# RG-LRU gate products of a hybrid decoder trunk: block-diagonal 128x128 weights replaced by 64x64 quadrants

## The chip, the core and the metric

The kernel runs on one NeuronCore of one Trainium2 chip. The metric is the device time of one execution in microseconds (us). Before the change the median of three runs was 1516.97 us (1516.93 to 1519.11). TensorE (PE in the rows; PEld its weight loads) multiplies into PSUM, VectorE (DVE) and ScalarE (ACT) work elementwise, SyncE (SP) issues transfers.

## The reference, cut to what matters

One step of a two-layer trunk, 1024 prompt positions and 8 decode tokens side by side (1032 columns), width 1024. Layer 0 holds an SSD mixer and a chunked gMLP, layer 1 a Conformer convolution module (C) and a Griffin RG-LRU (D). The change is in D, whose two gates are block-diagonal products with 16 heads of 64 channels:

```python
xc, buf_new = _causal_dwconv(xd, conv_buf, conv_w, conv_b)          # 4 taps
xb = xf.reshape(bsz, L, D_HEADS, D_BLOCK)                           # 16 heads of 64
r = sigmoid(einsum('blhi,hij->blhj', xb, wa).reshape(bsz, L, W) + ba)
i = sigmoid(einsum('blhi,hij->blhj', xb, wx).reshape(bsz, L, W) + bx)
log_a = -LRU_C * r * softplus(-lam)
a = exp(log_a);  bterm = sqrt(-expm1(2 * log_a)) * (i * xf)
h[t] = a[t] * h[t-1] + bterm[t]                                     # a scan over t
```

All arrays are fp32. C is a gated product, a causal convolution of 31 taps, a layer norm over the channels and SiLU; both branches are gated and go into one output projection.

## The kernel before, in words

Channels lie on the 128 partitions and the 1032 columns along the free axis, so each width of 1024 is eight blocks of 128 channels, and each block of D holds two heads. A large projection is a *unit* (line 120): 128 output channels in three column chunks of 344. `chunk` (line 107) writes one PSUM bank with 24 products: the fp32 operands are split into a high and a low part, and for each of eight contraction blocks lines 115 to 117 multiply high by high, high by low and low by high. The bank is then evacuated by ScalarE, or by VectorE for `ga` (line 827) and the output passes (line 732). `load_w` (line 93) brings a unit's weights, casts the high part on ScalarE (line 103) and subtracts on VectorE (line 104), at a raised priority of 700.

PSUM has eight banks of 512 fp32 columns: four under the tag "mm", which the chunks use, two under "sA" and two under "sB" for transposes, norms and gates (`bank`, line 59).

The program is written for a planner (the tile framework). It orders each engine's instructions by priority (program order, moved by `high_priority`) and by the times that its own timeline gives them, allots the slots of each tag, and places the semaphores. The engines then run these fixed orders, each waiting for what its next instruction needs.

Layer 1 runs as c, d, c, d and so on for eight blocks each (lines 903 to 905).

- `c_block(j)` (line 820): units `gb` and `ga`, the gated product `gl`, and `conv31` (line 841): 30 passes of VectorE over the block, one for each tap (line 859), 240 in all. They are put at priority -4000 and so fill what VectorE has left. `cacc` (line 865) sums the results over the blocks.
- `d_block(j)` (line 869): unit `xd` into `rwd`; `conv4` (line 291), one pass of ScalarE (line 294), three long passes of VectorE (line 297) and three of 8 columns for the decode tokens (line 300), into `xc`; unit `gd`; the gates; then the scan.

The gates before: two weight tiles `bd` (lines 809 to 818), each for four blocks, are zeroed by VectorE (line 812) and get their 64x64 diagonal blocks by 32 loads on SP's queue (line 817). Per block there are six products, two gates by three chunks, each 128x128 by 344 columns into the two "sA" banks, and a sigmoid behind each:

```python
for m, (t, bn) in enumerate(((rw, "lru_ba"), (gi, "lru_bx"))):          # L880
    for c in range(3):
        pg = bank("sA", f"gt{j}{m}{c}")                                  # L883
        T.matmul(pg[:, :CH], bd[:, m, j % 4, :], xc[:, cs], start=True, stop=True)
        S.activation(t[:, cs], pg[:, :CH], AF.Sigmoid, bias=pcol(bn, j)) # L885
```

In the trace a fp32 product is two instructions (passes), each with a weight load of its own.

After the eight blocks come eight units `gc`, meanwhile the results of D are reloaded (`mdl`) and split; then the output pass `od` over D (line 950) and `oc` over C (line 1013). While these run, the layer norm of C goes its way: the mean and the variance from `cacc` (lines 918 to 935), normalising and SiLU (lines 937 to 946), and the split into high and low operands, `hnh`/`hnl` for blocks 4 to 7 and `h_mc`/`l_mc` for blocks 0 to 3 (lines 949 and 953). `oc` multiplies blocks 4 to 7 first (k0=4). Its weights are `wh_oc`/`wl_oc`. After `oc` come the last norm and the outputs.

In layer 0 the SSD mixer has products of 64 output columns, `py` (lines 462 and 464): head h goes to PSUM partitions 0 to 63 or 64 to 127 by turns. `csT` (line 412) are products of 16 output columns, all on partitions 0 to 15. Both are fp32.

Of the kernel before, what the change touches and what calls it, by code (L numbers as in the profile page):

```python
# [10 lines left out]
AF = mybir.ActivationFunctionType  # L11
OP = mybir.AluOpType

P = 128
L = 1024
NS = 8
NT = L + NS
CH = NT // 3
NB = 8
# [4 lines left out]
RELU_ACT = 4  # L24
TPRI = 60
CPRI = 4000
ORDER = "cd" * 8

PROW = {}
# [15 lines left out]
def tile_trunk(ctx, tc, a, o):  # L45
    nc = tc.nc
    V, S, T, G, SY = nc.vector, nc.scalar, nc.tensor, nc.gpsimd, nc.sync
# [8 lines left out]
    def blk(tag, name, shape=None, dt=F32):  # L56
        return hp.tile(shape or [P, NT], dt, name=name, tag=tag, bufs=NTAG[tag])

    def bank(tag, name):
        return pp.tile([P, 512], F32, name=name, tag=tag, bufs=4 if tag == "mm" else 2)  # L60
# [59 lines left out]
    def unit(src, xs, name, evac, k0=0):  # L120
        w = load_w(src, name)
        for c in range(3):
            chunk(w, xs, c, name, evac, k0)
# [5 lines left out]
    def act_evac(dst, func, **kw):  # L129
        def f(ps, cs):  # L130
            S.activation(dst[:, cs], ps, func, **kw)  # L131
        return f

    def copy_evac(dst):
        def f(ps, cs):
            S.copy(dst[:, cs], ps)
        return f
# [43 lines left out]
    xts, ws = [], []  # L181
    for c in range(9):
# [7 lines left out]
        if c in (2, 3):  # L190
            col = XC + 1024 + (c - 2) * 256
# [46 lines left out]
    sc = cp.tile([P, NB, SR_BC], F32, name="sc")  # L238

    def pcol(name, j, k=0):  # L240
        return pc[:, j, PROW[name] + k:PROW[name] + k + 1]
# [38 lines left out]
    def tail_rows(t, lo, n, name, *outs):  # L280
        ps = bank("sA", "tl_" + name)
        T.transpose(ps[:n, :P], t[:, lo:lo + n], ident)
        rows = rowt("rows_" + name)
        S.copy(rows[:n], ps[:n, :P])
        i = 0
        for dst in outs:
            m = dst.shape[0]
            SY.dma_start(dst, rows[i:i + m])
            i += m

    def conv4(rw, dst, w, bcol, srow, j):
        pw, pb = PROW[w], PROW[bcol]
        col = lambda k: pc[:, j, pw + k:pw + k + 1]
        S.activation(dst, rw, AF.Identity, bias=pc[:, j, pb:pb + 1], scale=col(3))
        for k in range(3):
            d = 3 - k
            V.scalar_tensor_tensor(dst[:, d:L], rw[:, :L - d], col(k), dst[:, d:L], op0=OP.mult, op1=OP.add)
        st = sc[:, j, srow:srow + 24].rearrange("p (b k) -> p k b", k=3)
        for k in range(3):
            V.scalar_tensor_tensor(dst[:, L:], st[:, k, :], col(k), dst[:, L:], op0=OP.mult, op1=OP.add)  # L300

    def x_post(rw, col, j, bc, dst, name):
        conv4(rw, dst, "bc_w" if bc else "ssd_conv_w", "bc_b" if bc else "ssd_conv_b", S_BC if bc else S_SSD, j)
        S.activation(dst, dst, AF.Silu)
        tail_rows(rw, L - 3, 11, name, o["ssd_conv_prompt"][0, 0, :, col:col + P], o["ssd_conv_sample"][0, :, 2, col:col + P])
# [377 lines left out]
    def z_unit(j):  # L683
        t = blk("mt", f"sz{j}")
        unit(w_in_e[:, ZC + j * P:ZC + (j + 1) * P], hn, f"z{j}", act_evac(t, AF.Silu))
        V.tensor_mul(xy[j], xy[j], t)
        S.activation(t, xy[j], AF.Square)
        return t
# [13 lines left out]
    for g in range(2):  # L702
        acc = None
        for i in range(4):
            t = z_unit(g * 4 + i)
# [8 lines left out]
        for i in range(4):  # L714
            j = g * 4 + i
# [90 lines left out]
    V.tensor_scalar(cvec[:, :, 0], spl, -8.0, None, op0=OP.mult)  # L806
    V.tensor_scalar(cvec[:, :, 1], spl, 8.0, None, op0=OP.mult)

    bds = []
    for q, tag in enumerate(("S", "ws")):  # L810
        bd = blk(tag, f"bd{q}", [P, 2, 4, P])
        V.memset(bd, 0.0)
        for m, wn in enumerate(("lru_wa", "lru_wx")):
            for e in range(2):
                src = a[wn]
                for i in range(4):
                    SY.dma_start(bd[e * 64:(e + 1) * 64, m, i, e * 64:(e + 1) * 64], src[0, 2 * (q * 4 + i) + e])
        bds.append(bd)

    def c_block(j):  # L820
        sb = blk("xy", f"gl{j}")
        wb = load_w(w_in_o[:, GBC + j * P:GBC + (j + 1) * P], f"gb{j}")
        wa = load_w(w_in_o[:, GAC + j * P:GAC + (j + 1) * P], f"ga{j}")
        eb = act_evac(sb, AF.Sigmoid)

        def ea_(ps, cs):
            V.tensor_mul(sb[:, cs], ps, sb[:, cs])
        if j == 0:
            for c in range(3):
                chunk(wb, hn, c, f"gb{j}", eb)  # L830
                chunk(wa, hn, c, f"ga{j}", ea_)
        else:
            for c in range(3):
                chunk(wb, hn, c, f"gb{j}", eb)
            for c in range(3):
                chunk(wa, hn, c, f"ga{j}", ea_)
        js = slice(j * P, (j + 1) * P)
        tail_rows(sb, L - 30, 38, f"cc{j}", o["ccv_prompt"][0, 0, :, js], o["ccv_sample"][0, :, 29, js])
        conv31(j, sb)

    def conv31(j, gl):
# [13 lines left out]
        V.tensor_add(c[:, L:], c[:, L:], rd)  # L855
        with tc.high_priority(-CPRI):
            for k in range(29, -1, -1):
# [11 lines left out]
    def d_block(j):  # L869
        js = slice(j * P, (j + 1) * P)  # L870
        rw = blk("mt", f"rwd{j}")
        unit(w_in_o[:, XDC + j * P:XDC + (j + 1) * P], hn, f"xd{j}", copy_evac(rw))
        tail_rows(rw, L - 3, 11, f"lc{j}", o["lru_conv_prompt"][0, 0, :, js], o["lru_conv_sample"][0, :, 2, js])
        xc = blk("mt", f"xc{j}")
        conv4(rw, xc, "lru_conv_w", "lru_conv_b", S_LRUC, j)
        sgd = blk("ld", f"sgd{j}")
        unit(w_in_o[:, GDC + j * P:GDC + (j + 1) * P], hn, f"gd{j}", act_evac(sgd, AF.Silu))
        gi = blk("xx", f"gi{j}")
        bd = bds[j // 4]
        for m, (t, bn) in enumerate(((rw, "lru_ba"), (gi, "lru_bx"))):  # L880
            for c in range(3):
                cs = slice(c * CH, (c + 1) * CH)
                pg = bank("sA", f"gt{j}{m}{c}")  # L883
                T.matmul(pg[:, :CH], bd[:, m, j % 4, :], xc[:, cs], start=True, stop=True)
                S.activation(t[:, cs], pg[:, :CH], AF.Sigmoid, bias=pcol(bn, j))  # L885
        r = rw
        V.tensor_mul(gi, gi, xc)
        av = xc
        S.activation(av, r, AF.Exp, scale=cvec[:, j, 0:1])
        S.activation(r, r, AF.Tanh, scale=cvec[:, j, 1:2])  # L890
        hv = blk("mt", f"hv{j}")
        S.activation(hv, av, AF.Square)
        V.scalar_tensor_tensor(r, hv, 1.0, r, op0=OP.add, op1=OP.mult)
        S.activation(r, r, AF.Sqrt)
        V.tensor_mul(gi, gi, r)
        V.tensor_tensor_scan(hv[:, :L], av[:, :L], gi[:, :L], 0.0, op0=OP.mult, op1=OP.add)
        V.tensor_mul(hv[:, L:], av[:, L:], sc[:, j, S_LRU:S_LRU + NS])
        V.tensor_add(hv[:, L:], hv[:, L:], gi[:, L:])
        tail_rows(hv, L - 1, 9, f"lh{j}", o["lru_prompt"][0, :, js], o["lru_sample"][0, :, js])
        V.tensor_mul(hv, hv, sgd)  # L900
        SY.dma_start(mdd[j], hv)

    cj, dj = iter(range(NB)), iter(range(NB))
    for ch in ORDER:
        c_block(next(cj)) if ch == "c" else d_block(next(dj))
    sgc, md, mc = [], [None] * 8, [None] * 8
    for j in range(NB):
        t = blk("xy" if j < 7 else "S", f"sgc{j}")
        unit(w_in_o[:, GCC + j * P:GCC + (j + 1) * P], hn, f"gc{j}", act_evac(t, AF.Silu))
        sgc.append(t)  # L910
        if j >= 4:
            i = j - 4
# [9 lines left out]
    for i, j in enumerate((4, 5, 6, 7, 0, 1, 2, 3)):  # L922
        t = blk(("xy", "ce")[i % 2], f"cq{j}")
# [13 lines left out]
    for j in (4, 5, 6, 7, 0, 1, 2, 3):  # L937
        if j < 4:
            t = blk("bc", f"cr{j}")
            SY.dma_start(t, ccd[j])  # L940
            V.tensor_sub(t, t, mean)
        else:
            t = cs_t[j]
# [102 lines left out]
```

## Time and profile before

| | before |
|---|---|
| median of 3 runs | 1516.97 us (1516.93 to 1519.11) |
| profiled execution, first to last instruction | 1515.8 us (the profile shows nothing around it) |
| TensorE busy | 1497.5 us (99%), 9844 products |
| VectorE busy | 1058.3 us (70%) |
| ScalarE busy | 702.7 us (46%) |
| TensorE's granted clock, mean | 0.999 |

Busy time is the share of the span in which an engine ran an instruction. Products are pipelined: a record of TensorE is longer than the time to the next one's start, so what a product costs is read from starts, not from durations. In a timeline several equal instructions are merged (x4), with the start of the first and the time from there to the end of the last. "Idle before" says how long an engine waited and for whom. A line can be a helper's, so tiles are told by their names.

### The profile page before, as it was taken

The page shows a single profiled execution, that of the slowest core. Times are in us where ns is not written, and L with a number is a line of the kernel's source. Part 1 is how long each engine was busy: PE and PEld are TensorE (multiplying, and loading weights), DVE is VectorE, ACT ScalarE, POOL GpSimd, SP SyncE. Part 2 cuts the span into 40 slices and gives each one's busy share as a digit, 9 for nine tenths or more (in the row PEclk, how much of TensorE's full clock was granted, in tenths as well). Part 3 has the DMA queues.
Part 4 walks back from the last instruction along what each step waited for, and adds up shares of the span by engine and source line. Part 5 has one row for each costly group of instructions (what it writes and reads, how often), then busy time and mean ns, then how long its engine had stood idle before and what let it go on. Part 6 is the DMA issues. An engine that isn't in the chain of part 4 may idle for free.

```text
span 1515.8 us, 23657 instructions
## 1 busy us (share of the span) xinstructions
PE 1497.5 (99%) x9844; PEld 1464.1 (97%) x9844; DVE 1058.3 (70%) x1486; ACT 702.7 (46%) x1049; POOL 0.9 (0%) x7
## 2 busy tenths in 40 slices
PE   7999999999999999999999999999999999999998
PEld 6899999999999999999999999999999999999997
DVE  6535666568767862542437799999999999867524
ACT  6557666585654333420224445354445447334213
POOL 0000000000000000000000000000000000000000
PEclk9999999999999999999999999999999999999999
DMA  6225322233325661244432212221121221457402
GB/s 199 70 75 141 117 76 85 68 125 113 112 98 173 210 198 53 70 160 148 157 96 91 57 46 84 74 75 60 57 75 45 66 62 54 156 183 235 156 28 113
DMA packets 180193, 161.52 MB, mean 107 GB/s; under 512 B 11624, under 2 KB 159772, under 8 KB 180054
## 3 DMA queue, kind: packets, MB, share of 16 engines
q1 hardware_dynamic: 180086, 160.01, 33.5%
q8 instruction: 77, 1.26, 0.3%
q14 instruction: 30, 0.25, 0.1%
HBM read 118.91 MB, written 42.18 MB: 106 GB/s over the span
## 4 chain that ended last, share of the span: by engine, by line
PE 97%; ACT 1%; DVE 1%; DMA 0%; issue 0%; SPq 0%; DVEq 0%
PE mm_x L115 2%; PE mm_xd L115 2%; PE mm_x L117 2%; PE mm_xd L117 2%; PE mm_ob L116 2%; PE mm_od L115 2%; PE mm_z L115 2%; PE mm_oa L115 2%; PE mm_z L117 2%; PE mm_x L116 2%; PE mm_od L116 2%; PE mm_gd L115 2%; PE mm_u L115 2%; PE mm_ob L115 2%; PE mm_g L115 2%; PE mm_oc L115 2%
## 5 line engine op out<-in xcount | busy, mean ns | idle before, releaser
L859 DVE SCALAR_TENSOR_TENSOR c<-gl,pc,c 128x1017 f32<-128x1017 f32 (+25 forms) x240 | 294.7, 1262 | 0.9
L116 PE MATMUL mm_gb<-hnl,wh_gb 128*128 128x344 f32 x192 | 63.5, 331 | 0.3 <-DVE hnl L127 0.3
L115 PE MATMUL mm_gb<-hnh,wh_gb 128*128 128x344 f32 x192 | 63.1, 329 | 0.3 <-ACT gl L131 0.3
L115 PE MATMUL mm_xd<-hnh,wh_xd 128*128 128x344 f32 x192 | 62.6, 326 | 0.7 <-ACT wh_xd L103 0.7
L115 PE MATMUL mm_ga<-hnh,wh_ga 128*128 128x344 f32 x192 | 63.3, 329 | 0.0
L115 PE MATMUL mm_u<-hnh,wh_u 128*128 128x344 f32 x192 | 62.6, 326 | 0.0
L117 PE MATMUL mm_gb<-hnh,wl_gb 128*128 128x344 f32 x192 | 62.4, 325 | 0.0
L115 PE MATMUL mm_v<-hnh,wh_v 128*128 128x344 f32 x192 | 62.4, 325 | 0.0
L117 PE MATMUL mm_ga<-hnh,wl_ga 128*128 128x344 f32 x192 | 62.4, 325 | 0.0
L117 PE MATMUL mm_v<-hnh,wl_v 128*128 128x344 f32 x192 | 62.2, 324 | 0.0
L116 PE MATMUL mm_v<-hnl,wh_v 128*128 128x344 f32 x192 | 62.1, 324 | 0.0
L116 PE MATMUL mm_ga<-hnl,wh_ga 128*128 128x344 f32 x192 | 62.1, 324 | 0.0
L116 PE MATMUL mm_gc<-hnl,wh_gc 128*128 128x344 f32 x192 | 62.0, 323 | 0.0
L117 PE MATMUL mm_x<-hnh,wl_x 128*128 128x344 f32 x192 | 62.0, 323 | 0.0
L115 PE MATMUL mm_gc<-hnh,wh_gc 128*128 128x344 f32 x192 | 61.9, 323 | 0.0
L117 PE MATMUL mm_xd<-hnh,wl_xd 128*128 128x344 f32 x192 | 61.9, 324 | 0.0
L115 PE MATMUL mm_x<-hnh,wh_x 128*128 128x344 f32 x192 | 61.9, 322 | 0.0
L117 PE MATMUL mm_gd<-hnh,wl_gd 128*128 128x344 f32 x192 | 61.8, 322 | 0.0
L116 PE MATMUL mm_x<-hnl,wh_x 128*128 128x344 f32 x192 | 61.8, 322 | 0.0
L116 PE MATMUL mm_u<-hnl,wh_u 128*128 128x344 f32 x192 | 61.7, 321 | 0.0
L115 PE MATMUL mm_g<-hnh,wh_g 128*128 128x344 f32 x192 | 61.7, 321 | 0.0
L116 PE MATMUL mm_g<-hnl,wh_g 128*128 128x344 f32 x192 | 61.7, 321 | 0.0
(476 smaller groups left out, 4932.5 us busy)
## 6 DMA issues: line engine op xcount, KB each, us to landing
x<-res SPq DMA_DIRECT2D x16, 516.0 KB
csb<-csd SPq DMA_DIRECT2D x16, 512.0 KB
mbd<-u SPq DMA_DIRECT2D x8, 516.0 KB
mbl<-mbd SPq DMA_DIRECT2D x8, 516.0 KB
rb<-res SPq DMA_DIRECT2D x8, 516.0 KB
res<-rb SPq DMA_DIRECT2D x8, 516.0 KB
res<-x SPq DMA_DIRECT2D x8, 516.0 KB
mdd<-hv SPq DMA_DIRECT2D x8, 516.0 KB
```

The lines of the kernel that those rows point to most:

```text
L115: T.matmul(out, wh[:, k, :], xh[:, cs], start=i == 0, stop=False)
L116: T.matmul(out, wh[:, k, :], xl[:, cs], start=False, stop=False)
L117: T.matmul(out, wl[:, k, :], xh[:, cs], start=False, stop=i == NB - 1)
L859: V.scalar_tensor_tensor(c[:, d:L], gl[:, :L - d], w(k), c[:, d:L], op0=OP.mult, op1=OP.add)
```

## The change

Each gate product of 128x128 with two zero blocks becomes two products of 64x64, one for each head. The tile `gwt` holds the blocks without zeros and is filled by four loads. A block's twelve products stand one after another at a priority raised by 200 and write six banks: two of "mm", two of "sB", two of "sA". Row half e of the operands writes the bank e of its chunk; gate a goes to the same half of the output partitions, gate x to the other one. Twelve sigmoids of 64 partitions read them, those of gate a first. In `conv4` the three short passes go ahead of the three long ones.

```diff
+GPRI = 200
@@ conv4
+        st = sc[:, j, srow:srow + 24].rearrange("p (b k) -> p k b", k=3)
+        for k in range(3):
+            V.scalar_tensor_tensor(dst[:, L:], st[:, k, :], col(k), dst[:, L:], op0=OP.mult, op1=OP.add)
         for k in range(3):
             d = 3 - k
             V.scalar_tensor_tensor(dst[:, d:L], rw[:, :L - d], col(k), dst[:, d:L], op0=OP.mult, op1=OP.add)
-        st = sc[:, j, srow:srow + 24].rearrange("p (b k) -> p k b", k=3)
-        for k in range(3):
-            V.scalar_tensor_tensor(dst[:, L:], st[:, k, :], col(k), dst[:, L:], op0=OP.mult, op1=OP.add)
@@ weights of the gates
-    bds = []
-    for q, tag in enumerate(("S", "ws")):
-        bd = blk(tag, f"bd{q}", [P, 2, 4, P])
-        V.memset(bd, 0.0)
-        for m, wn in enumerate(("lru_wa", "lru_wx")):
-            for e in range(2):
-                src = a[wn]
-                for i in range(4):
-                    SY.dma_start(bd[e * 64:(e + 1) * 64, m, i, e * 64:(e + 1) * 64], src[0, 2 * (q * 4 + i) + e])
-        bds.append(bd)
+    gwt = blk("S", "gwt", [P, 2, NB, 64])
+    for m, wn in enumerate(("lru_wa", "lru_wx")):
+        src = a[wn][0].rearrange("(j e) i o -> e i j o", e=2)
+        for e in range(2):
+            SY.dma_start(gwt[e * 64:(e + 1) * 64, m], src[e])
+
+    def gates(j, xc, r, gi):
+        rows = [slice(e * 64, (e + 1) * 64) for e in range(2)]
+        pgs = [[bank(tag, f"gt{j}{c}{e}") for e in range(2)] for c, tag in enumerate(("mm", "sB", "sA"))]
+        with tc.high_priority(GPRI):
+            for c in range(3):
+                cs = slice(c * CH, (c + 1) * CH)
+                for m in range(2):
+                    for e in range(2):
+                        T.matmul(pgs[c][e][rows[e ^ m], :CH], gwt[rows[e], m, j, :], xc[rows[e], cs], start=True, stop=True)
+        for m, (t, bn) in enumerate(((r, "lru_ba"), (gi, "lru_bx"))):
+            for c in range(3):
+                cs = slice(c * CH, (c + 1) * CH)
+                for e in range(2):
+                    S.activation(t[rows[e], cs], pgs[c][e][rows[e ^ m], :CH], AF.Sigmoid, bias=pcol(bn, j)[rows[e]])
@@ d_block
-        bd = bds[j // 4]
-        for m, (t, bn) in enumerate(((rw, "lru_ba"), (gi, "lru_bx"))):
-            for c in range(3):
-                cs = slice(c * CH, (c + 1) * CH)
-                pg = bank("sA", f"gt{j}{m}{c}")
-                T.matmul(pg[:, :CH], bd[:, m, j % 4, :], xc[:, cs], start=True, stop=True)
-                S.activation(t[:, cs], pg[:, :CH], AF.Sigmoid, bias=pcol(bn, j))
+        gates(j, xc, rw, gi)
```

## Rows read from the trace of the kernel before

**Rows 1.** The page: busy time (share of the span) by engine; the chain by engine.

```profile
PE 1497.5 (99%) x9844; PEld 1464.1 (97%) x9844; DVE 1058.3 (70%) x1486; ACT 702.7 (46%) x1049; POOL 0.9 (0%) x7
...
PE 97%; ACT 1%; DVE 1%; DMA 0%; issue 0%; SPq 0%; DVEq 0%
```

**Rows 2.** Tile `gt`: duration in ns min/median/max, first and last start in us, forms.

```profile
L884 PE MATMUL gt<-xc,bd x96: 450/452/459, 876.1 to 1256.7; 128*128 128x344 f32 x96
L885 ACT ACTIVATE rwd<-gt,pc x24: 541/548/552, 876.8 to 1252.7; 128x344 f32<-128x344 f32 x24
```

**Rows 3.** Timeline of TensorE at the first gate products: start, us, instruction.

```profile
876.07 1.32 PE L884 MATMUL gt<-xc,bd 128*128 128x344 f32 x4
876.97 0.58 PE L117 MATMUL mm_gb<-hnh,wl_gb 128*128 128x344 f32 x1
877.38 0.32 PE L115 MATMUL mm_gb<-hnh,wh_gb 128*128 128x344 f32 x1
```

**Rows 4.** Timelines of TensorE at `py` and `csT`; last, `py`'s weight loads by tile.

```profile
157.59 0.32 PE L115 MATMUL mm_C<-hnh,wh_C 128*128 128x344 f32 x1
157.84 1.09 PE L462 MATMUL py<-csb,x 128*64 128x128 f32 x16
158.86 0.50 PE L470 MATMUL pn<-x,bth 128*128 128x512 f32 x1
...
75.52 1.05 PE L412 MATMUL csT<-tri,dA 128*16 128x128 f32 x8
...
L462 PEld LDWEIGHTS py<-csb,x x256: 132/137/137, 157.8 to 450.3; 128*64 128x64 f32 x128
```

**Rows 5.** Timeline of ScalarE around the first block's sigmoids.

```profile
873.90 1.05 ACT L103 CAST wh_ga<-wr_ga 128x1024 fp32r<-128x1024 f32 x1 [3.17 <-PE mm_gd L116]
875.33 1.28 ACT L885 ACT_TABLE_LOAD   x1
878.99 0.46 ACT L131 ACTIVATE gl<-mm_gb 128x344 f32<-128x344 f32 x1 [1.02 <-PE mm_gb L117]
```

**Rows 6.** Busy time in stretches of 50 us, then PEclk, DMA share, GB/s.

```profile
870.00:920.00 50.00, 50.00 (x311) 48.61 (x310) 47.83 (x48) 25.48 (x34) 0.00 (x0) 1.00 0.25 78
1120.00:1170.00 50.00, 50.00 (x311) 48.59 (x311) 48.34 (x50) 23.55 (x33) 0.00 (x0) 1.00 0.22 67
1270.00:1320.00 50.00, 50.00 (x320) 49.93 (x319) 47.40 (x43) 21.36 (x30) 0.00 (x0) 1.00 0.40 125
```

**Rows 7.** The page's convolution group; timelines of VectorE and TensorE at block 5's gates.

```profile
L859 DVE SCALAR_TENSOR_TENSOR c<-gl,pc,c 128x1017 f32<-128x1017 f32 (+25 forms) x240 | 294.7, 1262 | 0.9
...
1130.71 0.22 DVE L300 SCALAR_TENSOR_TENSOR xc<-sc,pc,xc 128x8 f32<-128x8 f32 x1
...
1136.52 1.03 PE L884 MATMUL gt<-xc,bd 128*128 128x344 f32 x3
```

**Rows 8.** Timelines of VectorE, TensorE and ScalarE from `cacc` to the start of `oc`.

```profile
1323.22 1.23 DVE L865 TENSOR_TENSOR cacc<-cacc,c 128x1032 f32<-128x1032 f32 x1
...
1374.38 1.23 DVE L104 TENSOR_TENSOR wl_od<-wr_od,wh_od 128x1024 fp32r<-128x1024 f32 x1 [0.41 <-ACT wh_od L103]
...
1383.47 0.51 DVE L732 TENSOR_TENSOR rd<-mm_od,rd 128x344 f32<-128x344 f32 x1
...
1396.60 1.22 DVE L127 TENSOR_TENSOR hnl<-sgc,hnh 128x1032 fp32r<-128x1032 f32 x1
...
1413.56 4.66 DVE L127 TENSOR_TENSOR l_mc<-sgc,h_mc 128x1032 fp32r<-128x1032 f32 x4
...
1409.35 0.32 PE L115 MATMUL mm_oc<-hnh,wh_oc 128*128 128x344 f32 x1
...
1415.00 0.64 PE L115 MATMUL mm_oc<-h_mc,wh_oc 128*128 128x344 f32 x3
...
1417.52 0.32 PE L116 MATMUL mm_oc<-l_mc,wh_oc 128*128 128x344 f32 x1
...
1409.43 1.05 ACT L103 CAST wh_oc<-wr_oc 128x1024 fp32r<-128x1024 f32 x1 [1.42 <-PE mm_od L116]
1410.39 3.91 ACT L126 CAST h_mc<-sgc 128x1032 fp32r<-128x1032 f32 x4
```

**Rows 9.** Tile `bd`: loads on SP's queue and the memsets, as in rows 2.

```profile
L817 SPq DMA_DIRECT2D bd<-in_lru_wa_dram x16: 475/594/728, 827.1 to 842.4; - x16
L812 DVE MEMSET bd<- x2: 912/912/912, 826.2 to 827.3; 128x1024 f32 x2
```

## The prediction

> **What bounds the kernel now.** I read the busy shares first, then the chain that ended last, then the gate products by their tile and in the order of time, then the other engines around them. TensorE is busy for 1497.5 of 1515.8 us and 97% of the chain is TensorE [rows 1]: a TensorE instruction taken away shortens the run, unless something else has been hiding just behind it. The gate products are 96 instructions (48 products, two passes each) [rows 2]. Four of them start at 876.07; the next projection product but one starts at 877.38, and a projection product takes 0.157 (36 of them lie between 1409.35 and 1415.00 [rows 8]), so four passes hold TensorE for 1.31 - 0.157 = 1.15 us, 0.289 us each [rows 3]. That is two cycles a column for 344 columns at the granted full clock. In all 96 x 0.289 = 27.7 us, all on the path: 3.47 us in each of the eight blocks.
>
> The second thing to see is VectorE: busy 47.8, 48.3 and 47.4 of 50 us in stretches from 870 to 1320 us [rows 6], because the 240 convolution passes of line 859 [rows 7], 30 to a block and put last in priority, fill every gap. It is nearly a second bound.
>
> **The change part by part.**
>
> *Products.* A block's 6 products (12 passes) become 12 quadrant products (24 passes), each with the same 344 columns, so 0.289 us each. What a block costs depends on how many run at once. No row shows 64-row operands. The nearest rows are those of `py`: 64 output columns, alternately in the lower and the upper column half. Sixteen passes of 128 columns span 1.09 us; less the 0.27 of the last record, that is 15 steps of 0.055. Eight `csT` passes, all in one column half, have steps of (1.05 - 0.27) / 7 = 0.111 for the same 128 columns [rows 4]. So two column halves do run beside each other. The ends for a block: one at a time 24 x 0.289 = 6.94; two at a time 3.47; four at a time 1.73. I take four: the row halves read different partitions, and the change gives each row half a PSUM bank of its own.
>
> Changing between whole-array and divided products costs something: `py` starts 0.25 after the product before it instead of 0.157, and the product after its last pass (157.84 + 1.09 - 0.27 = 158.66) starts 0.20 later instead of 0.11 [rows 4], together 0.19 per block if the twelve stay together. New cost 1.73 + 0.19 = 1.92, saved 3.47 - 1.92 = 1.55 per block, **12.4 us** in all on TensorE.
>
> The Trainium skill (TensorE: Matmul & The Clock Gate, "What overlaps and what doesn't") says that a weight load overlaps running matmuls only where its row group differs. By that rule loads within a row half would stand between the passes. The `py` passes share all rows, and a pair's 0.11 has no room for a load recorded at 0.137 [rows 4], so this trace does not bear the rule out.
>
> *Sigmoids.* Six of 0.548 us on 128 partitions [rows 2] become twelve on 64. No row has the narrow form; between half (0.27) and the whole I take the whole, since a row of the same length streams as many columns. That adds 6 x 0.55 = 3.3 us of ScalarE per block, where it is busy about 24 of 50 us [rows 6]. Hidden beside the projections; what it delays is the release of the banks (a rival below) and `gi`, which nothing soon needs.
>
> *Banks.* Two of the four "mm" banks, both "sB" and both "sA" are held per block. A projection chunk is 24 x 0.157 = 3.8 us and uses one mm bank. The first two banks are free after the eighth sigmoid: about 0.6 + 1.28 (table load [rows 5]) + 8 x 0.55 = 6.3 us. The other two mm banks take 7.6 us of products. I cost this at nothing; the cover is thin.
>
> *Weights.* 32 loads of about 0.59 us on SP's queue and two memsets of 0.91 us on VectorE go; four loads come [rows 9]. The loads are between 4 x 0.48 = 2 and the old 19 us. Either way they land well ahead of 876, with the weight loads queued behind them on SP earlier, not later. Zero: the projections hide it. The "ws" slot set free has no waiting user; zero, and the memsets' 1.8 us are spent before the convolution backlog exists.
>
> *conv4 order.* The three small passes (0.22 us) go ahead of the three long ones. Same instructions; `xc` may be ready up to 0.7 us sooner or later per block, against a lead of 5.6 (below). Zero.
>
> *What is late next.* The convolution passes end with `cacc` at 1323.22. From there a chain of layer norm work leads to the operands of pass `oc`: `hnl` 1397.8, `h_mc` from 1411.4 to 1414.3, `l_mc` up to 1418.2 [rows 8]. TensorE reaches `oc` at 1409.35 and needs `l_mc` at 1417.52, where it had first done other chunks' products on `hn`: this is met with little to spare. VectorE's work before `cacc` does not shrink, so the chain stays where it is while TensorE comes 12.4 us sooner, at 1397.0. Then four open banks give 4 x 12 x 0.157 = 7.5 us of `hn` products, to 1404.5, and TensorE waits for `h_mc`. With the chain unmoved the four chunks' remaining 48 products end shortly after 1418.2, at about 1418.2 + 4 x 0.157 = 1418.8. Now they end at 1409.35 + 96 x 0.157 = 1424.4. So the gain left is **5.6 us**; 6.8 are given back.
>
> Bounds of the chain's shift: 2.8 later (TensorE ahead pulls one more unit's VectorE work, 1.23 + 3 x 0.51 [rows 8], in front of `cacc`), or up to 6.8 sooner if VectorE's waits go. Some of these are waits for TensorE, as the 1.42 us of ScalarE before `wh_oc` at 1409.43 [rows 8]. I take no shift.
>
> *Sum.* The profiled span of 1515.8 lies 1.2 below the median of the runs, 1516.97; I carry the 1.2. 1516.97 - 12.4 + 6.8 = **1511.4**, this case's own range 1504.6 to 1514.2.
>
> **The rivals.**
>
> *The order no longer fits (same to slower).* The planner writes VectorE's queue by its own costs. Should it count the 24 passes one after another, it sees 6.9 us where it now sees 3.5, and puts three more convolution passes (3 x 1.17 us) per block ahead of that block's `xc`. In block 5 `xc` is ready at 1130.9 and used at 1136.5, a lead of 5.6 [rows 7]; it is gone after two blocks, and TensorE then waits for `xc`. A block is 12 x 3.77 + 3.47 = 48.7 us on TensorE; VectorE's 47.8 per 50 is 46.6 in it, plus 3.5 = 50.1, so 8 x 1.4 - 5.6 = about +5 us: 1522, between 1517 and 1525. The later passes then have less to wait for, so no loss at `oc`. For it: VectorE's share. Against: it needs a wrong cost that no row shows. 0.20.
>
> *Banks (slower).* At a block's twelve, if ScalarE puts all twelve sigmoids, the table load and two casts of 1.05 [rows 5] ahead of the next chunk's evacuation (0.46), the bank returns after 6.6 + 1.3 + 2.1 + 0.5 = 10.5 us against 7.6 of cover: 2.9 us idle a block, 23 in all, 1516.97 - 12.4 + 23 = 1527.6. It turns slower where the loss passes 1.55 us a block. For it: two banks fewer. Against: ScalarE is half idle, and the needed banks come back at the eighth sigmoid. 0.12.
>
> *Only two at a time.* 3.47 + 0.19 per block: +1.5, 1518.5. `py` shows no more than two. 0.08.
>
> *One after another* (the change does not do what it says): 6.94 + 0.19 - 3.47 = 3.66 per block, 1546. `py` speaks against. 0.05.
>
> *Weight loads exposed within a row half.* 12 loads of 0.137 per row half, the halves side by side, add 1.6 per block: 3.6 against 3.47, 1518. This is what the skill's rule on row groups would do. 0.03.
>
> **How the numbers follow.** The forecast has 0.52. About 0.2% (3 us) is what a measurement here can tell from no change: faster is below 1513.9, slower above 1520. Faster: 0.50 (the forecast, without its upper end). Same: 0.02 + 0.08 (the order, where it costs little) + 0.08 + 0.03 = 0.21. Slower: 0.12 (the order otherwise) + 0.12 + 0.05 = 0.29. The range from 1504 to 1526 takes in the forecast's bounds, the order and most of the banks' case; it leaves out 0.05 for one after another and some 0.08 more.
>
> **What would show it.** Gate passes in groups of 24 that take about 1.9 us (four at a time), 3.5 (two) or 6.9 (one); blocks some 1.5 us shorter on TensorE; VectorE still about 95% busy and `cacc` still near 1323; TensorE waiting on `h_mc` or `l_mc` for some 5 to 7 us at the start of `oc`. Waits of gate passes on `xc` would speak for the order; waits of `mm_gb` or `mm_ga` on a sigmoid or an evacuation, for the banks. I am wrong if TensorE's path shrinks by 12 us with no wait at `oc` (about 1505), or if the twelve do not overlap at all.

## The result and the profile after

The changed kernel takes 1576.5 us (1575.6 to 1577.1) against 1516.97: ratio 1.039, 95% interval 1.038 to 1.040. It is slower, and above the predicted range. The profiled execution spans 1574.7 us, 58.9 more than before. The line numbers have moved by up to some 15.

The page after the change: busy time by engine, the chain by engine, and one of the costliest groups (busy us, mean ns).

```profile
PE 1504.5 (96%) x9940; PEld 1469.2 (93%) x9940; DVE 1061.7 (67%) x1484; ACT 737.9 (47%) x1103; POOL 0.9 (0%) x7
...
PE 80%; ACT 9%; DVE 8%; issue 2%; DMA 0%; SPq 0%; DVEq 0%; ACTq 0%
...
L117 PE MATMUL mm_ga<-hnl,wh_ga 128*128 128x344 f32 x192 | 67.6, 352 | 0.0
```

TensorE now sits idle for 1574.7 - 1504.5 = 70.2 us, where it was 18.3 [rows 1]: 51.9 more. The other 7.0 are busy time, although the gates became cheaper, and a projection product has a mean of 352 ns in `mm_ga` where `mm_u` shows 321 to 326 on the same page. Both come from the same waits, as the rows below show. TensorE's waits after the change (what it waited for: us in total, times, longest):

```profile
PE tl_lh L283 <- DVE hv L907: 41.1, 8, 6.8
PE gt L828 <- DVE xc L301: 9.9, 6, 3.2
```

Neither wait was there before. The first is of a product that the change doesn't touch: `tl_lh`, the transpose of the last rows of the scan's result `hv`. Block 3 on TensorE (start, us, instruction, idle before it and releaser):

```profile
1038.47 0.32 PE L118 MATMUL mm_gd<-hnh,wl_gd 128*128 128x344 f32 x1
1040.64 1.97 PE L828 MATMUL gt<-xc,gwt 64*64 64x344 f32 x24 [1.84 <-DVE xc L301]
1042.53 0.43 PE L116 MATMUL mm_gb<-hnh,wh_gb 128*128 128x344 f32 x1
...
1057.27 0.32 PE L116 MATMUL mm_ga<-hnh,wh_ga 128*128 128x344 f32 x1
1063.12 0.37 PE L283 MATMUL tl_lh<-ident,hv 128*9 128x128 f32 x1 [5.54 <-DVE hv L907]
...
1063.59 0.49 PE L118 MATMUL mm_ga<-hnh,wl_ga 128*128 128x344 f32 x1
1063.87 0.49 PE L116 MATMUL mm_ga<-hnh,wh_ga 128*128 128x344 f32 x1
```

All 24 passes stand together and take 1.97, so four run at once, as predicted. But the gates now come straight behind the last product of `gd`, with no projection between, in all eight blocks; before, 14 to 173 projections stood there. They wait for `xc`; then 94 products and 15 us later TensorE stands still for `hv`, with 50 ready products of `ga` behind the transpose in its queue. VectorE and ScalarE in the same stretch:

```profile
1039.21 1.27 DVE L301 SCALAR_TENSOR_TENSOR xc<-rwd,pc,xc 128x1023 f32<-128x1023 f32 x1
...
1041.54 7.82 DVE L874 SCALAR_TENSOR_TENSOR c<-gl,pc,c 128x1016 f32<-128x1016 f32 x6
...
1060.64 2.28 DVE L905 TENSOR_TENSOR_SCAN hv<-xc,gi 128x1024 f32<-128x1024 f32 x1
1062.84 0.14 DVE L907 TENSOR_TENSOR hv<-hv,gi 128x8 f32<-128x8 f32 x1
```

```profile
1041.52 1.28 ACT L833 ACT_TABLE_LOAD   x1 [1.45 <-PE gt L828]
1042.81 0.54 ACT L833 ACTIVATE rwd<-gt,pc 64x344 f32<-64x344 f32 x1
...
1049.52 1.28 ACT L898 ACT_TABLE_LOAD   x1
```

From the gates to `hv` it is 1062.98 - 1040.64 = 22.3 us: twelve sigmoids up to 1049.5, four passes of ScalarE with table loads between them, and VectorE's part of the chain, with eleven convolution passes put among it. Before, `hv` came later still, 26 to 36 us behind the first gate product, but 117 to 191 products stood between the last gate product and the transposes, so that TensorE never waited there.

What a stall does to the clock stands in the busy time by stretch (from:to, length, busy of PE, PEld, DVE, ACT, POOL, then the granted clock, DMA share, GB/s):

```profile
1043.00:1057.00 14.00, 14.00 (x91) 14.00 (x90) 13.57 (x12) 13.73 (x19) 0.00 (x0) 1.00 0.12 36
1060.00:1063.00 3.00, 0.00 (x0) 0.00 (x0) 3.00 (x4) 1.34 (x3) 0.00 (x0) 0.59 0.00 0
1063.00:1066.00 3.00, 2.88 (x11) 2.91 (x12) 3.00 (x3) 0.26 (x1) 0.00 (x0) 0.50 0.00 0
1069.00:1072.00 3.00, 3.00 (x21) 3.00 (x20) 2.96 (x4) 0.00 (x0) 0.00 (x0) 1.00 0.28 109
```

During the 5.5 us in which TensorE did nothing the granted clock fell to 0.50, the level of 1.2 GHz, and stayed there behind the stall: products start 0.28 to 0.29 apart (1063.59, 1063.87 and on) instead of 0.157. So a stall is paid for twice.

VectorE over the whole stage shows what gave way:

```profile
1020.00:1070.00 50.00, 42.62 (x270) 41.08 (x269) 48.19 (x46) 27.03 (x38) 0.00 (x0) 0.93 0.22 67
1320.00:1370.00 50.00, 50.00 (x320) 50.00 (x319) 6.14 (x5) 11.56 (x20) 0.00 (x0) 1.00 0.18 53
```

It is as full as before [rows 6], but with other work. Convolution passes started before the gates of blocks 0 to 7 (counted in the trace): 12, 39, 65, 90, 118, 144, 173, 202 before; 12, 38, 67, 97, 127, 157, 187, 217 after. From block 2 on that is 30 a block: every block's whole convolution is done inside one round of the loop, no backlog is left for the time behind the last gates, where VectorE is now free (6.14 of 50 us), and a round takes 54 to 59 us instead of 49 to 56.

### The profile page after: what moved, and what is told of

The parts are those of the page before. It is cut to its first block, busy times and chain, and to the rows that moved or that the text cites. A ratio compares the mean times of both kernels' runs of the same rounds, so it can differ in the third digit from the quotient of the medians.

```text
span 1574.7 us, 23857 instructions
## 1 busy us (share of the span) xinstructions
PE 1504.5 (96%) x9940; PEld 1469.2 (93%) x9940; DVE 1061.7 (67%) x1484; ACT 737.9 (47%) x1103; POOL 0.9 (0%) x7
## 4 chain that ended last, share of the span: by engine, by line
PE 80%; ACT 9%; DVE 8%; issue 2%; DMA 0%; SPq 0%; DVEq 0%; ACTq 0%
DVE c L874 4%; PE mm_x L116 2%; PE mm_x L118 2%; PE mm_ob L117 2%; PE mm_od L118 2%; PE mm_z L116 2%; PE mm_od L116 2%; PE mm_oa L116 2%; PE mm_z L118 2%; PE mm_x L117 2%; PE mm_oc L116 2%; PE mm_ob L116 2%; PE mm_u L116 2%; PE mm_g L116 2%; PE mm_oa L118 2%; PE mm_oa L117 2%
## 5 line engine op out<-in xcount | busy, mean ns | idle before, releaser
L874 DVE SCALAR_TENSOR_TENSOR c<-gl,pc,c 128x1015 f32<-128x1015 f32 (+20 forms) x240 | 299.4, 1265 | 2.7
L117 PE MATMUL mm_ga<-hnl,wh_ga 128*128 128x344 f32 x192 | 67.6, 352 | 0.0
L118 PE MATMUL mm_ga<-hnh,wl_ga 128*128 128x344 f32 x192 | 67.5, 352 | 0.0
L116 PE MATMUL mm_ga<-hnh,wh_ga 128*128 128x344 f32 x192 | 66.6, 347 | 0.0
L118 PE MATMUL mm_gc<-hnh,wl_gc 128*128 128x344 f32 x192 | 62.6, 326 | 0.0
L118 PE MATMUL mm_u<-hnh,wl_u 128*128 128x344 f32 x192 | 61.6, 321 | 0.0
L116 PE MATMUL mm_z<-hnh,wh_z 128*128 128x344 f32 x192 | 61.6, 321 | 0.0
```

The costliest lines, as they stand in the source:

```text
L116: T.matmul(out, wh[:, k, :], xh[:, cs], start=i == 0, stop=False)
L117: T.matmul(out, wh[:, k, :], xl[:, cs], start=False, stop=False)
L118: T.matmul(out, wl[:, k, :], xh[:, cs], start=False, stop=i == NB - 1)
L874: V.scalar_tensor_tensor(c[:, d:L], gl[:, :L - d], w(k), c[:, d:L], op0=OP.mult, op1=OP.add)
```

## The experiments

The theory: the two banks taken from "mm" are what costs. Slots of a tag are allotted in program order. With two of the gates' banks between the chunks of `gd` and of `gb`, no chunk of `gb` comes ahead of a block's gates, and TensorE is tied to `xc` in each block. The counts in the traces bear this out: no projection stands between `gd` and the gates, in any block, in the changed kernel and the four others below that have the gates' banks at this place, and 14 to 194 in those whose gates take none from "mm". Before, the gates slid back behind up to 173 projections, and VectorE lived on that lead. Rivals: the raised priority, the quadrants with their twelve sigmoids, the order in `conv4`, the length of the chain to `hv`.

**The priority.**

```diff
-GPRI = 200
+GPRI = 0
```

> The changed kernel with the products' raised priority set to 0, all else kept. Theory (the two banks taken from the projections' tag tie the projections to the gates of their block; the priority has no part in it): within 3 us of the changed kernel's 1576.5, TensorE waiting some 41 us in all for hv and some 10 us for xc as in the changed kernel. Rival (the raised priority pulls the gates forward onto xc): the waits for xc and for hv fall below 10 us together, and the time goes to 1505 to 1520.

Measured: 1576.7 us, the waits the same.

```profile
PE tl_lh L283 <- DVE hv L907: 42.5, 8, 6.8
PE gt L828 <- DVE xc L301: 9.8, 5, 2.6
```

The raised priority has no part in it.

**Quadrants without "mm".**

```diff
-enumerate(("mm", "sB", "sA"))
+enumerate(("sA", "sB", "sA"))
```

> The changed kernel with its first pair of banks taken from sA instead of the projections' tag mm (so sA, sB, sA), the raised priority kept. Theory (the mm banks are the cause): projection chunks stand between gd and the gates again, TensorE's waits for xc and hv fall from 51 us to under 10, the granted clock returns to about 0.99 or more, and the time is 1505 to 1522: 1517 less the 12 to 13 us of gate time, plus up to 5 for passes that no longer stay together and up to 7 given back at oc. Rival (the quadrants or the twelve narrow sigmoids are the cause, whatever bank they use): the waits for hv stay above 25 us and the time above 1550.

Measured: 1516.7 us, ratio 0.9995 (0.9985 to 1.0004). Of TensorE's two waits one is left:

```profile
PE tl_lh L283 <- DVE hv L907: 1.0, 1, 1.0
```

The banks are the cause: the same quadrants and sigmoids on other banks, 15 to 112 projections between `gd` and the gates again, and 60 us are gone. That it is the place of the banks and not their number, the later runs show. Nothing was won over the kernel before, though. Four banks hold only eight of the twelve products, so the passes come in groups of 16, 4 and 4. TensorE at block 1's gates:

```profile
926.95 0.32 PE L117 MATMUL mm_gb<-hnl,wh_gb 128*128 128x344 f32 x1
927.20 1.39 PE L828 MATMUL gt<-xc,gwt 64*64 64x344 f32 x16
928.52 0.42 PE L118 MATMUL mm_gb<-hnh,wl_gb 128*128 128x344 f32 x1
928.78 0.32 PE L116 MATMUL mm_gb<-hnh,wh_gb 128*128 128x344 f32 x1
```

The first group takes 928.78 - 926.95 - 2 x 0.157 = 1.52 us: four steps of 0.289 and 0.36 for the two changes between whole and divided products. The groups of four passes (both products on one row half, so two at a time) take 0.92 each by the same reckoning. 1.52 + 2 x 0.92 = 3.36 against 3.47 before: the switching eats the gain.

**The transposes later.** In the changed kernel:

```diff
-        tail_rows(hv, L - 1, 9, f"lh{j}", ...)
+        with tc.high_priority(-150):
+            tail_rows(hv, L - 1, 9, f"lh{j}", ...)
```

> The changed kernel with one edit: the transposes of the last rows of hv are put 150 lower in priority, so that some 143 projection products instead of 95 stand between the gates and them. Theory (TensorE stands in order behind these transposes until hv is ready, 41 us in all, and the clock lost after it costs some 20 more): 48 more products at 0.157 are 7.5 us of cover against waits of at most 6.8, so the waits for hv vanish, the waits for xc stay at 10 us or grow somewhat, and the time is 1512 to 1535. Rival (the wait for hv only shows a lag of VectorE, which will be met elsewhere): as much idle time turns up in waits for xc or for banks, and the time stays within 15 us of 1576.

Measured: 1567.9 us, the rival's side. The wait for `hv` is gone and two others stand in its place:

```profile
PE tl_cc L283 <- DVE gl L842: 21.6, 7, 4.4
PE gt L828 <- DVE xc L301: 20.8, 7, 5.4
```

So the long chain to `hv` only decides where TensorE stands still. What it waits for is VectorE.

**The same with less for VectorE to do.** The kernel leaves out six taps of the convolution.

```diff
-            for k in range(29, -1, -1):
+            for k in range(29, 5, -1):
```

> The kernel of e3_late_tl with 24 of the 30 passes of the 31-tap convolution per block; six taps are left out, nothing else. In e3_late_tl the wait for hv had only moved: TensorE waited 21.6 us for gl and 20.8 us for xc, with VectorE some 95% busy. Theory, now in this form (in step with the gates VectorE has all 30 passes of a block to do in each round, about 53 us of work against 47.5 of TensorE, and TensorE waits for the difference): six passes of 1.26 us less are 45.5 us, below TensorE's, so the waits for gl, xc and hv fall below 10 us together and the time to 1502 to 1515. Rival (it is the length of the chain from the gates over the sigmoids and the scan to hv, whatever else VectorE has to do): the waits stay above 30 us and the time above 1550.

Measured: 1528.0 us, between the two expectations: 40 us less, with VectorE's busy time 55 us shorter (1060.4 to 1005.5).

```profile
PE tl_cc L283 <- DVE gl L842: 10.4, 7, 2.0
PE gt L828 <- DVE xc L301: 8.3, 6, 1.9
PE tl_lh L283 <- DVE hv L907: 1.6, 1, 1.6
```

VectorE's work is the larger part: the three waits fall from 42.4 to 20.3, and the clock is 0.998 again. But 1.4 to 1.5 us at a time remain for `xc` and for `gl`. VectorE has time to spare by then (46.4 of 50 us busy from 1020 to 1070), so these look like waits for single late results, which a TensorE tied to each block meets even so.

**Whole products on six banks.** The kernel before, with line 883's one bank for each product replaced:

```diff
+        pgs = [[bank(tag, f"gt{j}{c}{m}") for m in range(2)] for c, tag in enumerate(("mm", "sB", "sA"))]
...
+                    T.matmul(pgs[c][m][:, :CH], bd[:, m, j % 4, :], xc[:, cs], start=True, stop=True)
```

> The kernel before, with its whole 128x128 gate products (zero blocks kept, six sigmoids on 128 partitions), but all six products of a block side by side on six banks (mm, sB, sA) at the raised priority. Theory (the banks and the order they force are the cause, not the quadrants): no projection between gd and the gates, waits for xc of about 10 us in all as in the changed kernel; the chain from the gates to hv is 6 x 0.55 = 3.3 us shorter than with twelve sigmoids, so the waits for hv are 5.1 - 3.3 = some 2 us a block or less; with some clock lost the time is 1525 to 1550. Rival (the quadrants themselves and their twelve sigmoids are the cause): 1514 to 1520, as before.

Measured: 1545.4 us, ratio 1.019 (1.017 to 1.021), the theory's side. The banks cost 28 us without any quadrant. TensorE waits at the gates of seven blocks, 19.3 us in all, and for `hv` only 0.4:

```profile
PE gt L886 <- issue: 11.0, 3, 4.1
PE gt L886 <- ACT sgd L132: 5.4, 3, 2.1
PE gt L886 <- DVE xc L301: 2.9, 1, 2.9
```

The profile names three releasers, but the timeline shows one. In all seven blocks the first gate product starts 0.17 to 0.22 us after the start of the last short pass on `xc`, within 0.04 of its recorded end, whereas the last evacuation of `sgd` had ended 0.2 to 2.9 us before. Block 3:

```profile
1033.84 0.22 DVE L301 SCALAR_TENSOR_TENSOR xc<-sc,pc,xc 128x8 f32<-128x8 f32 x1
...
1034.02 0.91 PE L886 MATMUL gt<-xc,bd 128*128 128x344 f32 x1 [3.60 <-issue]
```

So they all read as waits for `xc`, twice what was expected. From block 2 on `hv` comes even later than in the changed kernel (24 to 27 us behind the first gate product, there 22 to 23), but 114 to 149 products stand between the last gate product and the transposes, there 86 to 97. That the kernel loses 28 us here and 59 with the quadrants goes with this; why the planner leaves more room here, whether for the six sigmoids or the longer gates, was not tried.

**Banks of their own.** "mm" is cut to two banks, a new tag "g" gets two:

```diff
-        return pp.tile([P, 512], F32, name=name, tag=tag, bufs=4 if tag == "mm" else 2)
+        return pp.tile([P, 512], F32, name=name, tag=tag, bufs=2)
...
-enumerate(("mm", "sB", "sA"))
+enumerate(("g", "sB", "sA"))
```

> The changed kernel with a pair of banks of its own for the gates: mm gets two banks instead of four, a new tag gets two, and the twelve products use that tag, sB and sA. All 24 passes of a block stand together and 14 to 92 projections stand between gd and them. Theory (not the quadrants and not their number side by side cost the time, but the tie of the projections to the gates through mm): no waits for xc or hv over 5 us in all, gates of 1.73 + 0.35 (two switches between whole and divided products, as the second look at e2_nomm's groups of 16 gives) = 2.1 us a block against 3.47, 11 us less on TensorE; with up to 7 given back at oc, where two open banks instead of four leave TensorE waiting, 1506 to 1514. Rival (two mm banks are too few for the projections, each evacuation leaves TensorE waiting): above 1520, with many waits for mm evacuations.

Measured: 1562.0 us: a miss, the rival came true. 14 to 92 projections stand between `gd` and the gates, and no wait for `xc` or `hv` is left, but the projections wait for evacuations from the start on (`mm_oa` begins at 742.1 instead of 731.0), the largest of them:

```profile
PE mm_ga L116 <- ACT gl L132: 10.3, 6, 2.4
PE mm_od L116 <- DVE rd L733: 7.0, 6, 2.1
```

So the tie can be undone and all twelve products kept together, but not by taking two banks from "mm" for good.

**The order in `conv4` alone**, in the kernel before.

```diff
+        for k in range(3):
+            V.scalar_tensor_tensor(dst[:, L:], st[:, k, :], col(k), ...)
         for k in range(3):
             d = 3 - k
             V.scalar_tensor_tensor(dst[:, d:L], rw[:, :L - d], col(k), ...)
-        for k in range(3):
-            V.scalar_tensor_tensor(dst[:, L:], st[:, k, :], col(k), ...)
```

> The kernel before with only the order of the short convolution's passes changed: the three small ones ahead of the three long ones. Theory (this part is worth nothing): within 2 us of before. Rival (it shifts the release of xc or the order behind it): a difference of 3 us or more.

Measured: 1516.6 us, ratio 0.9996 (0.9987 to 1.0005). Worth nothing, as predicted.

**Four banks, two groups.** In `gates`, chunks 0 and 1 take sA and sB, chunk 2 takes sA again later:

```diff
+        for g, tags in (((0, 1), ("sA", "sB")), ((2,), ("sA",))):
+            pgs = {c: [bank(tag, f"gt{j}{c}{e}") for e in range(2)] for c, tag in zip(g, tags)}
+            with tc.high_priority(GPRI if len(g) == 2 or j == 7 else -300):
```

> The changed kernel with its banks from sA and sB alone: eight of a block's twelve products side by side, the other four together some 100 projections later when the first pair of sA is free again (their priority is lowered for that). Theory (the loss came from the tie through mm; e2_nomm won nothing because its groups of 16, 4 and 4 passes cost 1.5 + 0.9 + 0.9 = 3.3 us a block against 3.47, each group paying some 0.35 for switching and the small ones running only two at a time): 1.5 + 0.93 = 2.4 us a block, 8 us less on TensorE than before; the work behind cacc then sets the end at oc, so 1509 to 1514, with waits of TensorE for h_mc or l_mc of 1 to 5 us. Rival (something else of the change eats the gain, as in e2_nomm): 1515 to 1519.

Measured: 1527.4 us, ratio 1.0065: a miss. The groups are as planned, but the projections between them now find their banks full, because ScalarE empties them behind the sigmoids:

```profile
PE mm_gd L116 <- ACT sgd L132: 8.0, 7, 1.1
PE mm_gb L116 <- ACT rwd L137: 5.4, 6, 0.9
```

**The same six banks, further on in the program.** `d_block` is cut ahead of the gates; the projections `gb` and `ga` of the next block are written in between (one unit of `gc` for the last block), the convolution and the transposes of that block behind the gates. The core of it:

```diff
+    for j in range(NB):
+        d = d_block(j)
+        nx = None
+        if j + 1 < NB:
+            nx = c_block(j + 1)
+        else:
+            gc_unit(0)
+        d_tail(j, *d, nx)
```

> The changed kernel with its six banks (mm, sB, sA), but with the gates of a block written behind the next block's gb and ga projections, so that 144 projections (22.6 us) stand between gd and them in every block; priority 0. Theory (mm banks as such cost nothing, the tie to xc does): all 24 passes together at 2.1 us a block, no waits for xc, hv or gl above 5 us in all, 11 us less on TensorE than before and up to 7 of them given back at oc: 1506 to 1513. Rival (two mm banks fewer after each group hold the projections up, or VectorE's 53 us of work a block hold TensorE whatever the order): waits of 20 us or more in the stage, 1525 or above.

Measured: 1517.4 us, ratio 1.0001 (0.9992 to 1.0010), between the two. In blocks 0 to 6 the gates come 48.0 us apart (895.3, 943.3, ... 1183.1), 24 passes together, and nothing waits. The last block alone, with 72 projections ahead instead of 144, gives it all back:

```profile
1227.28 3.72 PE L828 MATMUL gt<-xc,gwt 64*64 64x344 f32 x24 [7.31 <-DVE xc L301]
```

Here the 24 passes take 3.72, as the granted clock fell in the wait ahead of them (0.50 while they run); behind them `hv` is waited for 2.2 us.

**The same order with whole products.** `gates` as in the kernel before, on those banks.

```diff
-                        T.matmul(pgs[c][e][rows[e ^ m], :CH], gwt[rows[e], m, j, :], xc[rows[e], cs], start=True, stop=True)
+                T.matmul(pgs[c][m][:, :CH], bd[:, m, j % 4, :], xc[:, cs], start=True, stop=True)
```

> As e11_next_block, with the whole 128x128 products and their zero blocks of the kernel before in the place of the quadrants. It has the same order and the same banks, so its difference to e11_next_block is what the quadrants themselves are worth. If TensorE sets the end: 8 x (3.47 - 2.1) = 11 us more than e11_next_block. If the work behind cacc sets it, as the prediction's step on oc has it: 4 to 7 us more. Its own time 1514 to 1520.

Measured: 1525.0 us, above its own range and 7.6 more than with quadrants. By itself this would fit the step on `oc`; but both kernels wait for `xc` in the last block (6.6 and 7.3 us), and the next pair, without it, decides otherwise.

**Two units of `gc` ahead of the last gates.**

```diff
-            gc_unit(0)
+            for i in range(2):
+                gc_unit(i)
...
-        if j:
+        if j >= 2:
```

> As e11_next_block, with two units of gc instead of one ahead of the last block's gates, so that 144 projections stand between gd and the gates there too. In e11_next_block blocks 0 to 6 ran in 48.0 us each with no wait, and the last gates waited 7.3 us for xc, hv another 2.2, and the granted clock fell to 0.93 in that stretch, some 3.5 us more: about 13 us in all. Theory A (TensorE sets the end; the work behind cacc moves with it): 13 us less than e11_next_block, 1503 to 1507, with no wait at oc. Theory B (the step on oc of the prediction: the chain from cacc to l_mc stays where it is, and TensorE, 12 us sooner, waits there): 5 to 8 us less, 1509 to 1513, with waits for h_mc or l_mc of 4 to 7 us. If VectorE's backlog only moves the wait for xc to another place, 1515 to 1518.

Measured: **1504.9 us** (1504.7 to 1505.4), ratio 0.992 (0.991 to 0.994): faster than both kernels, 12.2 us below before and 71.6 below the changed kernel, with its quadrants, its banks and its number of products. Theory A. Its page:

```profile
PE 1485.0 (99%) x9940; PEld 1451.5 (97%) x9940; DVE 1055.5 (70%) x1484; ACT 720.1 (48%) x1092; POOL 0.9 (0%) x7
...
PE 97%; ACT 1%; DVE 1%; DMA 0%; issue 0%; SPq 0%; ACTq 0%; DVEq 0%
```

Against this run the loss of the changed kernel can be split, since TensorE has the same products to do in both: idle 70.2 - 18.1 = 52.1 us, and busy 1504.5 - 1485.0 = 19.5 us. Nearly all of the second part is the lowered clock: the changed kernel's TensorE was busy for 38.3 us at 0.50, this one's for none, and at 0.286 instead of 0.157 us a projection product that makes some 17 us (an estimate). TensorE at block 1's gates, and where it reaches `oc`; then VectorE's last `cacc` and `l_mc`, and its busy time in a stretch of the stage:

```profile
942.47 0.32 PE L118 MATMUL mm_ga<-hnh,wl_ga 128*128 128x344 f32 x1
942.72 1.97 PE L828 MATMUL gt<-xc,gwt 64*64 64x344 f32 x24
944.62 0.43 PE L116 MATMUL mm_xd<-hnh,wh_xd 128*128 128x344 f32 x1
944.88 0.32 PE L117 MATMUL mm_xd<-hnl,wh_xd 128*128 128x344 f32 x1
...
1396.49 0.32 PE L116 MATMUL mm_oc<-hnh,wh_oc 128*128 128x344 f32 x1
...
1308.10 1.23 DVE L883 TENSOR_TENSOR cacc<-cacc,c 128x1032 f32<-128x1032 f32 x1
1401.02 4.66 DVE L128 TENSOR_TENSOR l_mc<-sgc,h_mc 128x1032 fp32r<-128x1032 f32 x4
...
1020.00:1070.00 50.00, 50.00 (x331) 48.55 (x331) 50.00 (x51) 28.39 (x41) 0.00 (x0) 1.00 0.21 67
```

**And with whole products**, the same replacement as above.

> As e13_two_gc, with the whole products and zero blocks of the kernel before: the same order, without the quadrants. e12_next_whole was 7.6 us slower than e11_next_block, both with a wait of about 7 us for xc in the last block. Theory A (TensorE sets the end): 8 x 1.4 = 11 us more than e13_two_gc, 1514 to 1518. Theory B (the chain behind cacc sets it once the gates are quadrants): 4 to 7 us more than e13_two_gc, 1514 to 1518.

Measured: 1517.0 us, 12.1 more than with quadrants. So the new order by itself is worth nothing (1517.0 against 1517.1), and the quadrants in it are worth 12.1 us. VectorE's last `cacc` and `l_mc` here:

```profile
1322.87 1.23 DVE L882 TENSOR_TENSOR cacc<-cacc,c 128x1032 f32<-128x1032 f32 x1
...
1413.82 4.66 DVE L128 TENSOR_TENSOR l_mc<-sgc,h_mc 128x1032 fp32r<-128x1032 f32 x4
```

## Why the prediction was wrong

*Products: right.* Twenty-four passes in 944.88 - 942.47 - 2 x 0.157 = 2.10 us, taken as 1.92; the two switches cost 0.36 together instead of 0.19. Predicted 12.4 us less on TensorE; in an order that lets them count they gave 12.1: 8 x (3.47 - 2.10) = 11.0 in the stage, and 1.0 ahead of it (first gates at 894.8 against 895.8). That 12.1 comes so near to 12.4 is in part luck: a block gave 1.37 instead of 1.55, and the 1.0 is no part of that sum. *One after another* and *only two at a time* are out: four passes start within 0.02 us (942.721 to 942.741), the next four 0.34 and from then on 0.289 later. The weight loads, recorded at 0.13 each, find no room within a row half there. The Trainium skill (TensorE: Matmul & The Clock Gate, "What overlaps and what doesn't") lets a load overlap only where the row group differs; by that they would have shown, and the measurement decides against it here.

*Sigmoids: the size right* (0.542 on 64 partitions, the whole duration as taken), the cover not: `gi` was said to be what nothing soon needs. It is needed for `hv`, and `tl_lh` waits for that.

*Weights and the order in `conv4`: right*, nothing for `conv4` and at most that 1.0 us for the weights.

***Banks: the step that failed.*** It said "I cost this at nothing; the cover is thin". With the same quadrants and the same banks, gates placed 144 projections on made the kernel 71.6 us faster (1504.9 against 1576.5). The cover that it reckoned was of the banks' release: in the changed kernel no projection waits for that. What it left out is that the two banks are a place in an order. They stand between two chunks in "mm", so that they tie the stream of projections to `xc`, and the lead of 5.6 us and the slide of up to 173 projections, which the trace of before showed, are no longer there to hide anything. The runs without "mm" (1516.7), with the banks and no quadrants (1545.4) and with the same banks 144 projections on (1504.9) show it.

*The rival on the order* saw the place (VectorE's convolution passes, waits for `xc`) and priced it at 5 us, for three passes more a block over the lead. Its premise, a wrong price for the quadrants, is not what set it off, as the tie is there with whole products too (1545.4), and it lacked the two large terms: the wait for `hv`, 41.1 us, and the clock, some 17. *The rival on banks* was meant for evacuations; it didn't occur here, but it did in the runs with two "mm" banks and with two groups.

*The step on `oc` was wrong too*, though not to be seen in the time: the chain behind `cacc` was said to stay where it is, giving back 6.8 us. At 1504.9 us TensorE reaches `oc` 12.9 sooner than before (1396.49 against 1409.35 [rows 8]) and waits for nothing, as `cacc` comes 15.1 sooner (1308.10 against 1323.22) and `l_mc` 12.5. It is the quadrants that move them: with whole products in the same order they come at 1322.87 and 1413.82, nearly as before. VectorE was not full before: 47 to 48 of 50 us [rows 6], against up to 50.0 now. Between `cacc` and `l_mc` its queue holds the sums of `od`, which wait for TensorE (9.8 us in all in the kernel before) and move with it. The changed kernel shows that as well: its `cacc` comes at 1318.5, 4.7 sooner than before, but its `l_mc` only at 1466.0, two us ahead of `oc`, and nothing waits there either.

## What to carry to other kernels

A tile taken from a pool that another stream uses is a place in that stream's order, whatever its count of free slots says: before costing it at nothing, ask which instructions can no longer pass, and how far they slid past each other in the trace of before. Where a second engine is nearly full, the lead between the two is a resource; price its loss as the whole work of that engine in one round against the first engine's, and a stall of TensorE with the clock that it loses. If the operations are worth having, keep them and move the place in the program: here 144 projections turned a loss of 59.5 us into a gain of 12.2.

## What the runs showed of the hardware

- Behind a stall of 5.5 us the granted clock was at 0.50, and some fifteen products passed at half speed; against the fastest run, 52.1 us more of idle time brought 38.3 us of busy time at 0.50, some 17 us lost.
- Changing between whole 128x128 and 64x64 products costs 0.36 us for there and back (0.09 ahead of the group, 0.05 in its first step, 0.2 behind it), so that a group of four passes costs 0.92 us against 0.58 of steps. The Trainium skill (TensorEngine Tiling (Array Packing), "Key Properties") says that changing the tiling mode drains TensorE; the runs show a cost at each change and give it this price, but not that a drain is what costs.
- Passes of 64x64 quadrants in fp32 step at 0.289 us for 344 columns, the same as whole ones [rows 3], but four at once.
